# A decoder trunk step: the delta stage's projections, filler and head chain in another rank order, and the output branch's first banks

## The chip, the cores and the metric

The kernel runs on one core of one Trainium2 chip. The time is the device time of one execution in microseconds; three executions of the kernel before give a median of 2136.81 us (2132.54 to 2142.25). The engines are named as the profile names them: PE is TensorE (PEld its weight loads), DVE is VectorE, ACT is ScalarE, POOL is GpSimd and SP is SyncE, which issues most of the transfers.

## What is computed

One layer of a hybrid trunk for 1024 prompt tokens and 8 single-token samples, model width 1024, all in float32. Cut to what matters here:

```
h   = rmsnorm(x) * (1 + scale1) + shift1
qkv, gdn_gate, beta, a, sq, sk, sv, ga, gb = split(h @ w_in)

# gated delta rule, 8 heads of 128, chunks of positions, one after the other
q, k, v = silu(conv4(qkv))
for each head:
    T    = inverse(I + strictly_lower(beta k k^T * decay))      # per chunk
    for each chunk:                                             # a chain: S goes from chunk to chunk
        v_new = T (...v...) - T (...k...) S
        o     = q S + (q k^T * decay) v_new
        S     = S * last_decay + k^T v_new
y_a = (rmsnorm(o) * silu(gdn_gate)) @ w_gdn_out

o_b = sliding_window_attention(sq, sk, sv);  y_b = o_b @ w_swa_out
x   = x + gate1 * ((sigmoid(ga) * y_a + sigmoid(gb) * y_b) @ w_o)

h2  = rmsnorm(x) * (1 + scale2) + shift2
x   = x + gate2 * ((silu(conv3(h2 @ w_gate)) * (h2 @ w_up)) @ w_down)
y   = rmsnorm(x)
```

The states of the samples and the last rows of the caches are outputs too.

## The kernel before

**Products.** Every large product is made of three matmuls in a reduced float32 form: each operand is split into a high and a low part (`split`, L125: a copy on ACT, a subtraction on DVE), and `mm3` (L176) multiplies high by high, high by low and low by high (L178 to L180). A projection tile has 128 output columns. Its weights are loaded by SP (`load_split`, L130), and it runs over the 1032 tokens in three parts of 384, 384 and 264 columns; a part is 8 `mm3`, 24 matmuls, into one PSUM bank, which is then read out. `next_mm` (L172) goes round the list `self.mm` of bank pools: `pmm` has two banks and `pmf` one.

**Order.** Instructions carry a rank, `tc.cur_priority`, which counts up by one with each instruction that is written down. A planner puts each engine's instructions in order before the run: of those whose inputs and buffers are there in its own picture of time, it takes the one with the lowest rank. On the chip each engine then follows that fixed order. Buffers of one name in one pool are reused in the order in which the program asks for them. `issue_after` ties instructions of an engine behind a given one.

`weave` (L1248) writes several streams down one after the other but gives them overlapping ranks: a stream has a start and a step, and begins at the base `p` plus start. After each `yield`, a stream of step 1 counts on from where its instructions brought it, and a stream of another step is set to start plus so many steps. At the end the base for what follows is the largest rank that a counted stream has reached; before, streams with a start under 10000 are counted.

**The delta stage** (`run`, L1964 to L1982). For each of 8 heads one `weave` holds:

- `unit_inverse` (start 0, step 1): the triangular inverse of the head's 8 blocks. Transfers to DRAM and back (L987, L992, L1015, L1018), a loop of 15 pairs of small DVE operations (L1009, L1010), then rounds of small matmuls (L1028 to L1064) that write the tile `W`, of which there is one.
- `delta_scan` (100, step 1): 8 chunks, each a chain of three matmuls with ACT and DVE operations between them (L937 to L953). In the middle and at the end the output is normalized, turned and multiplied with the gate tile `sg`, which has one buffer for heads 0 to 6.
- `delta_prepare` of the next head (250, step 1): transposes, norms and the products of keys with keys and queries (L856 to L914).
- `head_projections`: for heads 0 to 5 the gate tile of head h (`delta_gate`, L840) and the three convolved tiles K, Q, V of head h+2 (`delta_project`, L784; `conv_tile`, L762). It is written behind two pieces of filler, as one stream with start 500 and step 100. All of it uses the two `pmm` banks.
- filler, `pieces` (L805): one piece is 8 steps of `self.filler`, one part of a tile. The filler is the 16 tiles of the two branch gates (`gates`, L1271; read out by L1284) and then an early piece of the output branch, 8 parts of 264 columns (`early_out`, L1294). Three pieces a head have start 10000 and step 100. Up to head 5 they use the bank `pmf` and a weight buffer of their own, of one copy.

Head 6 has three pieces and the gate tiles of heads 6 and 7 at start 500 in steps of 1, and nine more pieces at start 600; head 7 has what is left of the filler at start 600. From head 6 on filler and gates share `[pmm, pmm, pmf]`, and what is written after `delta_scan` is tied behind its steps by `spaced` (L164), two `mm3` to a step.

**The output branch** (`branches`, L1318) follows. Its products go round five banks, `[pmm, pmm, pmf, more, more]`, of which `more` is a new pool, laid where the delta stage's own small banks were. `turn`, the place in that round, is left as the delta stage had it. The first two products, j = 0 and 1 over the first 384 tokens, use rows that were loaded early.

**The second half** also has a `weave` (L1894): the output passes at step 1, and the states, norms and operands of the next part at steps of 10 to 120 with starts up to 730.

Of the kernel before, what the change touches and what calls it, by code (L numbers as in the profile page):

```python
# [62 lines left out]
class Step:  # L63
# [1184 lines left out]
    def weave(self, *streams):  # L1248

        tc = self.tc  # L1250
        p = end = tc.cur_priority
        for gen, start, step in streams:
            at = tc.cur_priority = p + start
            for _ in gen:
                if start < 10000:
                    end = max(end, tc.cur_priority)
                at += step
                tc.cur_priority = max(at, tc.cur_priority) if step == 1 else at
            if start < 10000:
                end = max(end, tc.cur_priority)  # L1260
        tc.cur_priority = end

# [661 lines left out]
    def run(self):  # L1924
        S, nc = ExitStack, self.nc
        self.constants()
        with S() as ca:
            with S() as c:
                pool, psum = self.pool("p2", 1, ctx=c), self.pool("q2", 1, PSUM, ctx=c)
                for tag, bufs in dict(qst=8, raw=2, kh=2, kl=2, E=3, obt=2, pp=2, pc=2, o=2).items():  # L1930
                    self.bufs[id(pool), tag] = bufs
                self.conditioning(pool, psum)
                self.vectors(pool, psum)
                self.h = self.new_parts()
                for lo in (8, 12, 0, 4):
                    self.modulation(pool, psum, "sc", lo, (("qst", 8),), "mrows")
                    if lo == 8:
                        self.junk = self.t(pool, [P, NP], "vch", bufs=1)
                        xs = self.norm_part(pool, self.load_rows(pool, 0, ("raw", "raw", "V")))
                    if lo == 12:  # L1940
                        self.a1 = self.norm_scale("a1", 8, self.n1w)
                        self.early = [self.win(COL_SK)]
                    if lo == 0:
                        self.early.append(self.win(COL_SQ))
                with self.tc.issue_after(self.mod_load.ins):
                    self.xs = {1: self.load_rows(pool, 1, ["qst"] * 3)}
                    self.junk = self.t(pool, [P, NP], "qst", bufs=8)
                    self.early.append(self.win(COL_SV, tags=("wmh", "wml"), home=pool))
                    self.early.append(self.win(COL_SQ + P, tags=("obt", "obt"), home=pool))
                self.xs[2] = self.load_rows(pool, 2, ("raw", "raw", "V"))  # L1950
                self.modulate_part(pool, psum, 0, xs, self.a1, 0)
                self.attention(pool, psum)
            cg = S()
            pgt = self.pool("pgt", 1, ctx=cg)
            self.pz, self.zs = self.pool("pz", 1, ctx=cg), True
            pg = self.pool("pg", 1, ctx=ca)
            self.fill_side = pg, 1, 1
            self.fill_where, self.gt = [self.fill_side], (pgt, "gt")
            with S() as c:
                pa, pool, psum = self.pool("pa", 1, ctx=c), self.pool("p4", 1, ctx=c), self.pool("q4", 1, PSUM, ctx=c)  # L1960
                self.W = self.t(pool, [P, NCH, P], "W", bufs=1)
                nc.gpsimd.memset(self.W, 0.0)
                self.kqv, self.sg = {}, {}
                self.weave((self.delta_project(pa, pool, 0), 0, 1))  # L1964
                self.weave((self.delta_prepare(pool, psum, 0), 0, 1), (self.delta_project(pa, pool, 1), 100, 1))
                for h in range(H):
                    if h + 2 == H:
                        self.fill_where, self.fill_psum = [self.fill_side, self.where], None
                        self.mm = [self.pmm, self.pmm, self.pmf]
                    prep = self.prep  # L1970
                    streams = [(self.unit_inverse(pool, psum, h, prep[0]), 0, 1),
                               (self.delta_scan(pool, psum, h, prep), 100, 1)]
                    if h + 2 < H:
                        streams[1:1] = [(chain(self.pieces(2), self.head_projections(pa, pool, h)), 500, 100)]
                        streams.append((self.pieces(3), 10000, 100))
                    else:
                        if h + 2 == H:
                            streams[1:1] = [(chain(self.pieces(3), *(self.delta_gate(pa, pool, i) for i in (h, h + 1))), 500, 1)]
                        streams.append((self.head_projections(pa, pool, h), 600, 100))
                    if h + 1 < H:  # L1980
                        streams.append((self.delta_prepare(pool, psum, h + 1), 250, 1))
                    self.weave(*streams)  # L1982
                    self.steps = []
                for _ in self.filler:
                    pass
            self.a2 = self.norm_scale("a2", 32, self.n2w)
        with S() as c:
            pool2, pool = self.pool("p6b", 1, ctx=c), self.pool("p6", 1, ctx=c)

            self.psm, more = self.pool("qs", 2, PSUM, ctx=c), self.pool("qb", 2, PSUM, ctx=c)  # L1990
            mm, self.mm = self.mm, [self.pmm, self.pmm, self.pmf, more, more]
            self.branches(pool, pool2)
            self.mm = mm
        cg.close()
        self.wctx.close()
        self.second_half()
# [40 lines left out]
```

## Time and profile before

| | us |
|---|---|
| median of three executions | 2136.81 (2132.54 to 2142.25) |
| profiled execution, its time | 2136.28 |
| its span, first to last instruction | 2134.5 |
| PE busy in the span | 2046.5 |
| DVE, ACT, POOL busy | 1393.5, 854.7, 534.6 |
| delta stage, about | 430 to 1155 |

Busy times are those of instructions on the engine; matmuls overlap each other, so a row's duration is longer than the distance from one start to the next. In a row of the timeline the text in brackets is the idle time just before the instruction and what ended it. In a row of a line's instructions stand the count, the least, median and greatest duration in ns, the first and the last start in us, and the shapes. A stretch's row has, for each engine, busy time and number of instructions, and then TensorE's granted clock as a share of full speed, the mean busy share of the DMA engines and the GB/s that they moved.

### The profile page before, as it was taken

Reading aid. Unit: us, or ns where it says so; the run is one execution under the profiler, and the core shown is the slowest. Engines: PE = TensorE matmul, PEld = TensorE weight load, DVE = VectorE, ACT = ScalarE, POOL = GpSimd, SP = SyncE. Lnnn points to the kernel's source line nnn. Section 1 sums busy time; section 2 is a strip of 40 time slices with the busy share of each in tenths; the row PEclk is TensorE's granted clock in tenths of the full one; section 3 lists DMA queues with packets and bytes.
Section 4 is the critical chain, followed back from the end, with each engine's and each line's share of the span. In section 5 each row is a group of like instructions: output and inputs, shape, how many; then the busy total and the mean of one; then the engine's idle time right before and its main releaser. Section 6 shows DMA issues by size and latency. Waiting matters only on the chain. (4 is left out here: it accounts for less than half of the span.)

```text
span 2134.5 us, 41210 instructions
## 1 busy us (share of the span) xinstructions
PE 2046.5 (96%) x16245; PEld 1935.3 (91%) x16245; DVE 1393.5 (65%) x2781; ACT 854.7 (40%) x2125; POOL 534.6 (25%) x592
## 2 busy tenths in 40 slices
PE   7999999999899999999989989998999999999898
PEld 4985888899899999999879989898999999999898
DVE  4756667465655736557445575479888788678866
ACT  3655445434244233443343222344343343343443
POOL 1000000020221211212110220003546546545531
PEclk8999999999999999999989999999999999999999
DMA  7256442141332322313166663622333333388972
GB/s 272 86 133 204 141 161 90 49 135 48 76 85 58 83 58 54 89 52 76 48 183 211 213 224 100 182 61 71 109 95 95 110 95 95 120 285 276 317 228 85
DMA packets 301821, 274.95 MB, mean 129 GB/s; under 512 B 59666, under 2 KB 248303, under 8 KB 301612
## 3 DMA queue, kind: packets, MB, share of 16 engines
q1 hardware_dynamic: 296140, 252.49, 38.6%
q0 software_dynamic: 5200, 19.32, 2.6%
q8 instruction: 127, 2.08, 0.4%
q14 instruction: 66, 0.54, 0.1%
q10 hardware_dynamic: 288, 0.52, 0.1%
HBM read 212.54 MB, written 62.12 MB: 129 GB/s over the span
## 5 line engine op out<-in xcount | busy, mean ns | idle before, releaser
L178 PE MATMUL mm<-b1h,wh 128*128 128x384 f32 (+1 forms) x1520 | 499.0, 329 | 5.9 <-ACT gt L1284 4.1
L180 PE MATMUL mm<-b1h,wl 128*128 128x384 f32 (+1 forms) x1520 | 491.4, 325 | 2.1 <-DVE wl L128 2.1
L179 PE MATMUL mm<-b1l,wh 128*128 128x384 f32 (+1 forms) x1520 | 490.8, 323 | 0.0
L178 PEld LDWEIGHTS mm<-b1h,wh 128*128 128x128 f32 x1520 | 287.8, 190 | 15.7 <-ACT gt L1284 6.2
L180 PEld LDWEIGHTS mm<-b1h,wl 128*128 128x128 f32 x1520 | 287.3, 189 | 7.9 <-issue 4.3
L179 PEld LDWEIGHTS mm<-b1l,wh 128*128 128x128 f32 x1520 | 288.0, 189 | 3.8 <-issue 3.5
L127 ACT ACTIVATE wh<-raw 128x1024 fp32r<-128x1024 f32 x83 | 87.0, 1048 | 135.7 <-PE mm L179 75.9
L128 DVE TENSOR_TENSOR wl<-raw,wh 128x1024 fp32r<-128x1024 f32 x82 | 100.8, 1229 | 48.8 <-ACT wh L127 47.9
L179 PE MATMUL mm<-pk,w 128*128 128x260 f32 (+1 forms) x440 | 124.3, 283 | 1.1 <-DVE pk L128 1.1
L178 PE MATMUL mm<-pk,w 128*128 128x260 f32 (+1 forms) x440 | 124.3, 283 | 0.0
L180 PE MATMUL mm<-pk,w 128*128 128x260 f32 (+1 forms) x440 | 124.2, 282 | 0.0
L128 DVE TENSOR_TENSOR w<-ws,w 128x512 fp32r<-128x512 f32 x88 | 74.1, 843 | 37.4 <-ACT w L127 37.4
L1609 ACT COPY bml<-mm 128x256 f32<-128x256 f32 (+1 forms) x132 | 49.2, 374 | 108.5 <-PE mm L180 101.8
L178 PE MATMUL mm<-bmh,w 128*128 128x260 f32 (+1 forms) x320 | 90.4, 283 | 0.9 <-DVE fa L1686 0.9
L180 PE MATMUL mm<-bmh,w 128*128 128x260 f32 (+1 forms) x320 | 90.3, 282 | 0.0
L180 PE MATMUL mm<-b2h,wl 128*128 128x384 f32 (+1 forms) x256 | 83.4, 329 | 4.5 <-DVE wl L128 4.5
L178 PE MATMUL mm<-b2h,wh 128*128 128x384 f32 (+1 forms) x256 | 83.8, 329 | 2.4 <-DVE t L1327 2.4
L179 PE MATMUL mm<-b2l,wh 128*128 128x384 f32 (+1 forms) x256 | 83.9, 328 | 0.4 <-DVE b2l L128 0.4
L179 PEld LDWEIGHTS mm<-pk,w 128*128 128x128 f32 x440 | 82.8, 188 | 1.3 <-DVE pk L128 1.3
L178 PEld LDWEIGHTS mm<-pk,w 128*128 128x128 f32 x440 | 82.8, 188 | 0.3 <-ACT bml L1609 0.2
L180 PEld LDWEIGHTS mm<-pk,w 128*128 128x128 f32 x440 | 83.0, 189 | 0.0
L127 ACT ACTIVATE w<-ws 128x512 fp32r<-128x512 f32 x88 | 55.4, 632 | 49.9 <-PE wv L180 45.0
(648 smaller groups left out, 5984.1 us busy)
## 6 DMA issues: line engine op xcount, KB each, us to landing
raw<-in_w_in_dram SPq DMA_DIRECT2D x60, 512.0 KB
ws<-in_w_ffn_down_dram SPq DMA_DIRECT2D x55, 256.0 KB
raw<-xd SPq DMA_DIRECT2D x47, 258.0 KB
raw<-in_w_ffn_down_dram SPq DMA_DIRECT2D x47, 256.0 KB
raw<-in_w_ffn_gate_dram SPq DMA_DIRECT2D x22, 512.0 KB
raw<-in_w_ffn_up_dram SPq DMA_DIRECT2D x22, 512.0 KB
qst<-in_w_mod_dram SPq DMA_DIRECT2D x16, 512.0 KB
raw<-in_w_mod_dram SPq DMA_DIRECT2D x16, 512.0 KB
```

The source lines that it names most:

```text
L127: self.nc.scalar.activation(hi, x, AF.Copy)
L128: (eng or self.nc.vector).tensor_tensor(lo, x, hi.bitcast(F32), op=ALU.subtract)
L178: mm(ps, whi, xhi, start=first, stop=False, **kw)
L179: mm(ps, whi, xlo, start=False, stop=False, **kw)
L180: self.last_mm = mm(ps, wlo, xhi, start=False, stop=last, **kw).ins
L1609: self.last_copy = nc.scalar.copy(r[p, i], x[p])
```

## The change

`weave` counts streams by their step instead of their start. In the delta stage five starts go to 100000: the projections' stream of heads 0 to 5 (with the two pieces at its front), the stream of three pieces and two gates of head 6, and the pieces of heads 6 and 7. Three pieces a head stay at 10000. The starts of the inverse, the scan and the preparation stay. Before the output branch `turn` is set to -1, so that its first product goes to the first bank of the list.

```diff
@@ weave
         for gen, start, step in streams:
             at = tc.cur_priority = p + start
             for _ in gen:
-                if start < 10000:
+                if step == 1:
                     end = max(end, tc.cur_priority)
                 at += step
                 tc.cur_priority = max(at, tc.cur_priority) if step == 1 else at
-            if start < 10000:
+            if step == 1:
                 end = max(end, tc.cur_priority)
@@ run
                     if h + 2 < H:
-                        streams[1:1] = [(chain(self.pieces(2), self.head_projections(pa, pool, h)), 500, 100)]
+                        streams[1:1] = [(chain(self.pieces(2), self.head_projections(pa, pool, h)), 100000, 100)]
                         streams.append((self.pieces(3), 10000, 100))
                     else:
                         if h + 2 == H:
-                            streams[1:1] = [(chain(self.pieces(3), *(self.delta_gate(pa, pool, i) for i in (h, h + 1))), 500, 1)]
-                        streams.append((self.head_projections(pa, pool, h), 600, 100))
+                            streams[1:1] = [(chain(self.pieces(3), *(self.delta_gate(pa, pool, i) for i in (h, h + 1))), 100000, 1)]
+                        streams.append((self.head_projections(pa, pool, h), 100000, 100))
...
-            mm, self.mm = self.mm, [self.pmm, self.pmm, self.pmf, more, more]
+            mm, self.mm, self.turn = self.mm, [self.pmm, self.pmm, self.pmf, more, more], -1
```

More of the change, by code (lines that the diff above doesn't have):

```diff
@@ L1977, in run @@
                         if h + 2 == H:
-                            streams[1:1] = [(chain(self.pieces(3), *(self.delta_gate(pa, pool, i) for i in (h, h + 1))), 500, 1)]
-                        streams.append((self.head_projections(pa, pool, h), 600, 100))
+                            streams[1:1] = [(chain(self.pieces(3), *(self.delta_gate(pa, pool, i) for i in (h, h + 1))), 100000, 100)]
+                        streams.append((self.head_projections(pa, pool, h), 100000, 100))
                     if h + 1 < H:
```

## The prediction

> **What bounds the kernel now.** I read the page first (busy shares, the slices of TensorE's clock), then the stretches of the delta stage, then what TensorE waited for there, then single places in the order of time. The page says that TensorE is the engine that counts:
>
> ```profile
> span 2134.5 us, 41210 instructions
> PE 2046.5 (96%) x16245; PEld 1935.3 (91%) x16245; DVE 1393.5 (65%) x2781; ACT 854.7 (40%) x2125; POOL 534.6 (25%) x592
> PEclk8999999999999999999989999999999999999999
> ```
>
> The change keeps every matmul, so only time in which TensorE stands still, or runs at a lower granted clock, can move. The edited stage runs from about 430 to 1155 us. By stretches (us; busy and count of PE, PEld, DVE, ACT, POOL; then granted clock, DMA share, GB/s):
>
> ```profile
> 430.00:540.00 110.00, 108.51 (x908) 106.29 (x907) 67.67 (x124) 42.33 (x123) 20.94 (x31) 1.00 0.33 91
> 540.00:570.00 30.00, 24.70 (x150) 23.17 (x148) 24.51 (x56) 8.64 (x22) 12.41 (x14) 0.94 0.38 95
> 570.00:1030.00 460.00, 452.31 (x4146) 437.55 (x4146) 264.93 (x566) 170.29 (x499) 81.51 (x120) 1.00 0.26 68
> 1030.00:1040.00 10.00, 7.30 (x43) 6.20 (x44) 4.13 (x9) 8.68 (x38) 1.30 (x2) 0.66 0.26 71
> 1040.00:1100.00 60.00, 59.78 (x525) 58.05 (x524) 31.26 (x90) 18.62 (x58) 12.63 (x20) 1.00 0.28 76
> 1100.00:1110.00 10.00, 5.22 (x84) 4.45 (x82) 6.31 (x8) 6.02 (x10) 1.77 (x2) 0.84 1.07 352
> 1110.00:1120.00 10.00, 6.47 (x44) 6.12 (x45) 1.66 (x3) 3.10 (x7) 0.00 (x0) 0.50 0.97 267
> 1120.00:1155.00 35.00, 34.32 (x275) 33.62 (x275) 19.73 (x39) 12.27 (x30) 4.57 (x6) 0.99 0.57 161
> sum 725.00, PE 698.61 PEld 675.44 DVE 420.21 ACT 269.95 POOL 135.14; mean PE 87.33 PEld 84.43 DVE 52.53 ACT 33.74 POOL 16.89
> ```
>
> Idle is 725 - 698.6 = 26.4 us. Where the clock is below 1, busy time times (1 - clock) is lost too: 24.70 x 0.06 = 1.5, 7.30 x 0.34 = 2.5, 5.22 x 0.16 = 0.8, 6.47 x 0.50 = 3.2 and 0.3 in the last row, 8.3 in all. So about 35 us, 1.6% of the time, is all that a better order can win. It is concentrated: 5.3 + 1.5 = 6.8 us at 540-570, 2.7 + 2.5 = 5.2 at 1030-1040, (4.8 + 3.5) + (0.8 + 3.2) = 12.3 at 1100-1120; the long steady part has 7.7 us in 460.
>
> Why 540-570 is thin: the gate projection of head 1 (L848 reads its three parts), the next convolution input (L770) and the filler (L1284):
>
> ```profile
> L848 ACT ACTIVATE th<-mm x3: 373/491/493, 533.6 to 614.4; 128x384 f32<-128x384 f32 x2, 128x264 f32<-128x264 f32 x1
> L770 ACT COPY z<-mm x1: 481/481/481, 620.4 to 620.4; 128x384 f32<-128x384 f32 x1
> L1284 ACT ACTIVATE gt<-mm x11: 372/482/493, 543.7 to 607.8; 128x384 f32<-128x384 f32 x7, 128x264 f32<-128x264 f32 x4
> ```
>
> Two parts of gate 1 are multiplied early and then sit in both projection banks until scan 0 gives `sg` back, so the third follows at 614; no projection runs meanwhile, and only filler, through one bank, is left. The gap at 1100-1120 is the other end of it: head 7's inverse comes after the gate filler has run out.
>
> ```profile
> 1103.57 0.28 PE L180 MATMUL mm<-b1h,wl 128*128 128x264 f32 x1
> 1108.00 1.45 PE L1051 MATMUL tp<-T,tmp 32*32 32x32 f32 x32 [4.15 <-ACT tmp L1048]
> 1112.19 1.94 PE L1060 MATMUL tp<-MR,UZ 64*64 64x64 f32 x16 [2.75 <-DVE MR L1057]
> 1114.80 1.96 PE L1064 MATMUL tp<-W,UZ 64*64 64x64 f32 x16 [0.67 <-ACT UZ L1061]
> 1117.43 0.80 PE L940 MATMUL rc<-vn,W 128*128 128x128 f32 x2 [0.67 <-ACT W L1065]
> ```
>
> **The chain of heads.** Starts of the eight inverses (L995), then the eight chunks of scan 5 and of scan 7 (L942; first and last start):
>
> ```profile
> L995 POOL COPY T<-unit x8: 289/292/294, 432.4 to 1032.1; 128x128 f32<-128x128 f32 x8
> L942 ACT ACTIVATE s<-rc,c x8: 362/368/375, 952.4 to 1030.1; 128x128 f32<-128x128 f32 x8
> L942 ACT ACTIVATE s<-rc,c x8: 358/368/369, 1118.3 to 1144.8; 128x128 f32<-128x128 f32 x8
> ```
>
> A head's period is (1032.1 - 432.4) / 7 = 85.7 us. Scan 5 takes 77.7 us for what scan 7, with far less beside it on VectorE, does in 26.5. `W` has one copy, so inverse h+1 can't finish before scan h; 77.7 and some 8 us of inverse make the whole period. The chain of small operations and TensorE's own work are of nearly one length, and at 1100 it is the chain that is late.
>
> **The change, part by part.**
>
> *Projections from +500 to +100000, no longer counted in the next base.* A head's base then grows by some 350 ranks, not 1100 (instructions counted in the code), so the small operations of heads 0 to 6 all stand ahead of every projection. Four tiles per head move. Each brings a load on SP, a split on ScalarE and VectorE, 72 matmuls and three copies; the three convolved ones also two small GpSimd operations, two tanh and six VectorE operations, three of them like L776:
>
> ```profile
> raw<-in_w_in_dram SPq DMA_DIRECT2D x60, 512.0 KB
> L776 DVE SCALAR_TENSOR_TENSOR K<-z,cw,K x21: 1266/1275/1287, 439.5 to 987.5; 128x1024 f32<-128x1024 f32 x21
> 551.03 0.34 PE L178 MATMUL mm<-b1h,wh 128*128 128x384 f32 x1
> 551.21 0.34 PE L179 MATMUL mm<-b1l,wh 128*128 128x384 f32 x1
> ...
> 1152.41 0.28 PE L179 MATMUL mm<-b1l,wh 128*128 128x264 f32 x1
> 1152.52 0.28 PE L180 MATMUL mm<-b1h,wl 128*128 128x264 f32 x1
> 1153.00 0.42 PE L178 MATMUL mm<-b1h,wh 128*128 128x384 f32 x1
> ```
>
> From start to start a matmul takes 0.18 us at 384 columns and 0.11 to 0.12 at 264: 24 x (0.18 + 0.18 + 0.12) = 11.5 us a tile, 3.8 us a filler part. None of it is added or removed. What moves ahead of it is the chain: on VectorE, the 15 pairs of the inverse now stand ahead of nine 1.28 us convolution steps a head, 11.5 us. SP's queue is passed by the inverse's loads as well; at a DMA share of 0.26 to 0.28 in the steady part I cost that at nothing, because weights have a second buffer and one tile hides 11.5 us of load. If that cover fails, the wait is again TensorE's.
>
> *Filler ahead of projections.* Three of five parts a head stand at +10000. The other two keep the front of the projections' chain, and filler shares one weight buffer and one bank, so parts run in program order: five parts of head h come before gate h and the tiles of h+2, then those of h+1. The price is order alone. For 540-570 it means that gate 1 comes behind up to 8 more filler parts, 8 x 3.8 = 30 us of the 80.8 between its first part and its third. I take half of 6.8: 3.5 us gained (bounds 0 and 6.8).
>
> *Steady part, 570-1030.* 7.7 us idle. With chunks no longer queued behind convolutions the chain runs ahead of TensorE, and projections stay in hand as cover; I take 2 us (bounds: a gain of 7.7, and the loss of the third case below).
>
> *Head 6 and 7.* Gates 6 and 7 with three parts go to +100000 in single steps, so head 7's base lies behind them; nine parts of head 6 and the early output parts go from +600 to +100000. Parts of head 6 stay tied behind scan 6's steps, those of the early output behind scan 7's, as before. At 1030-1040 both banks again wait for `sg`; with the chain ahead there are gates and parts to run: 4 us of 5.2 (bounds 0 and 5.2). At 1100-1120 the inverse of head 7 should be nearer its cover: after the last tile, 3 + 6 + 9 parts x 3.8 = 68 us and early output 64 x 3 x 0.12 = 23 us remain, 91 us and the small operations. Against it stands the chain of head 7: from the start of its inverse, 1032.1, to its scan, 1117.4, it took 85 us with its preparation and a hole of 13.6 us in it, so some 72 without the hole, and 26.5 of scan, 98 in all. That fits barely, so I take 8 of 12.3 (bounds 0 and 12.3).
>
> *The output branch's banks.* `turn = -1` puts its first two products into the two projection banks. In the rows above the first 384-column matmul follows the early output's last one after four transposes and no idle time; there is nothing to win in this order. A bank that comes free late would cost one part, 24 x 0.18 = 4 us, and cover of two parts may save 8: I take 0.
>
> *The other weave.* `end` now counts only streams of step 1, and the second half weaves too, with steps of 10 to 120: the first gate weights of the FFN and the last norm move up by some 450 ranks, ahead of the third norm's tail. There:
>
> ```profile
> 1450.00:1500.00 50.00, 43.86 (x352) 42.36 (x352) 47.57 (x67) 22.62 (x44) 24.88 (x23) 1.00 0.25 78
> ```
>
> 6.1 us idle, with VectorE at 95%: the same VectorE work in another order. I take 0 (bounds 6 either way).
>
> Sum: 3.5 + 2 + 4 + 8 = 17.5 us. The profiled execution took 2136.28 us (span 2134.5), 0.5 below the median: 2136.28 - 17.5 = 2118.8, against the median 2119.
>
> On the clock: the Trainium skill ("TensorE: Matmul & The Clock Gate", Part 1) says that TensorE falls to half rate after a window of about 3.4 us without work, and knows no value between. The 0.50 behind the 4.15 us gap agrees; the 0.66 at 1030-1040, where busy time is 7.3 of 10, would need such a gap and shows a thin stretch. By the rule alone the third term could be no more than its 2.7 us of idle time, and the sum would be 16.2.
>
> **The rivals.** What TensorE waited for between 430 and 1200 (total, times, longest):
>
> ```profile
> PE mm L178 <- ACT gt L1284: 4.1, 7, 1.3
> PE rc L940 <- DVE y L938: 1.8, 2, 1.1
> PE rc L944 <- ACT s L942: 1.6, 4, 0.6
> ```
>
> *The order hardly moves.* Projections wait for buffers that scans give back, filler for its one bank; program order within each buffer may leave the queue nearly as it is. For it: 452.31 busy of 460 in the steady part; against it: the banks held for 80 us. Then only about half of the first and third terms come, 2136 - 3 = 2133.
>
> *Small operations hold the queue.* TensorE takes its matmuls in order. A scan has 8 + 8 + 7 = 23 matmul steps that wait for ScalarE or VectorE, 184 in eight heads. Ranked above all else, each is put in as soon as the planner thinks its input is there; where the chip is later, everything behind waits. Now 6 of them wait, 3.4 us, 0.57 each. If a third (61) did, it would be 61 x 0.57 = 35 us, 2119 + 35 = 2154. It decides from 17.5 / 0.57 = 31 steps on. Against it: scans already ranked above their own head's projections, and waited 6 times. The Trainium skill ("PSUM — Partial Sum Buffer", Engine vs sequencer instructions) has the same rule, that matmuls start and finish in program order while weight loads may run ahead; the four gaps of the rows at 1108 to 1117 agree.
>
> *Head 7 comes later.* Filler that goes early can't cover late: if tile V of head 7 slips by the nine parts of head 6 (34 us) and the chain isn't ahead, the hole of 1117.4 - 1103.9 = 13.6 us grows to about twice itself: 2136 + 14 = 2150. For it: filler is now preferred to head 7's projections; against it: parts run in program order, so the same ones lie behind that tile.
>
> **How the numbers follow.** Forecast 0.46, own range 2104 (all of 6.8 + 7.7 + 5.2 + 12.3 = 32 us) to 2126 (10 us); order hardly moves 0.28; small operations hold the queue 0.16; head 7 later 0.10. A measurement of this kernel tells about 0.5%, 10.7 us, from no change. Faster by more is the forecast, 0.46; within it the second case, 0.28; slower the last two, 0.26. The range that should hold it 8 times in 10 is 2104 to 2150: it leaves out the upper part of the third case and little else.
>
> **What would show it.** Right: gate 1's three parts closer than 80.8 us; idle at 540-570 under 3 us; scans of the middle heads shorter than 77.7; no gap over 2 us between the last gate filler and the early output; 0.9 or more of clock in every stretch; the stage ends near 1137, and all after it is as long as before. Wrong: waits of L940 and L944 above 15 us together, or scan 7 beginning after 1117 with nothing beside it; or the second half, whose matmuls are the same, changing by more than 6 us.

## The result, and the profile after

The changed kernel takes 2124.68 us (median of six runs, 2121.29 to 2125.88), the kernel before 2134.27 beside it (2132.54 to 2142.25): a ratio of 0.9948, 95% interval 0.9931 to 0.9964. It is some 11 us faster (7.7 to 14.7). The prediction of 2119 had the direction and overstated the size.

One thing above is wrong. The diff in the section on the change, and the prediction's paragraph on heads 6 and 7, give head 6's stream of three pieces and two gates a step of 1. The change has step 100:

```diff
-                            streams[1:1] = [(chain(self.pieces(3), *(self.delta_gate(pa, pool, i) for i in (h, h + 1))), 500, 1)]
+                            streams[1:1] = [(chain(self.pieces(3), *(self.delta_gate(pa, pool, i) for i in (h, h + 1))), 100000, 100)]
```

So that stream isn't counted either, and head 7's base lies only some 350 ranks behind head 6's. The kernel as it was written there was run too, as e8.

The stretches of the changed kernel, with the same columns as the prediction's (engines' busy time and count, then granted clock, DMA share, GB/s); the 460 us from 570 also in four parts:

```profile
430.00:540.00 110.00, 108.33 (x912) 105.97 (x911) 60.91 (x116) 42.17 (x122) 22.10 (x33) 1.00 0.35 97
540.00:570.00 30.00, 30.00 (x203) 29.96 (x202) 22.38 (x57) 8.79 (x21) 11.54 (x14) 1.00 0.39 97
570.00:1030.00 460.00, 450.67 (x4122) 433.78 (x4120) 273.51 (x576) 174.40 (x507) 78.22 (x119) 0.99 0.25 66
570.00:930.00 360.00, 356.92 (x3318) 344.58 (x3316) 213.61 (x454) 135.37 (x397) 63.66 (x96) 1.00 0.26 69
930.00:950.00 20.00, 17.78 (x123) 16.03 (x116) 10.62 (x16) 11.55 (x39) 2.39 (x4) 0.84 0.11 31
...
1000.00:1030.00 30.00, 26.29 (x354) 24.33 (x352) 13.54 (x21) 10.12 (x22) 3.28 (x4) 1.00 0.20 57
1030.00:1040.00 10.00, 8.24 (x53) 7.51 (x54) 4.09 (x10) 8.46 (x43) 1.15 (x2) 0.66 0.34 111
1040.00:1100.00 60.00, 59.01 (x581) 56.46 (x580) 29.68 (x86) 17.01 (x50) 12.80 (x19) 1.00 0.25 64
1100.00:1110.00 10.00, 10.00 (x74) 9.55 (x72) 6.70 (x10) 6.70 (x11) 1.63 (x2) 1.00 0.94 305
1110.00:1120.00 10.00, 7.63 (x58) 6.82 (x56) 4.57 (x8) 3.26 (x5) 0.32 (x1) 1.00 1.19 307
1120.00:1155.00 35.00, 31.64 (x232) 30.39 (x233) 19.66 (x39) 12.63 (x30) 4.57 (x6) 1.00 0.75 224
```

540 to 570 is full, 1100 to 1110 is full; 1030 to 1040 is about as thin as it was; and there is a hole at 930 to 950 that the kernel before did not have there.

Rows of single lines in the changed kernel: the readouts of gate 1 (L848), the starts of the eight inverses (L995), and the chunks of scan 5 and of scan 7 (L942):

```profile
L848 ACT ACTIVATE th<-mm x3: 375/490/490, 571.1 to 620.6; 128x384 f32<-128x384 f32 x2, 128x264 f32<-128x264 f32 x1
...
L995 POOL COPY T<-unit x8: 289/289/291, 436.0 to 1029.8; 128x128 f32<-128x128 f32 x8
...
L942 ACT ACTIVATE s<-rc,c x8: 349/367/370, 950.2 to 1027.8; 128x128 f32<-128x128 f32 x8
...
L942 ACT ACTIVATE s<-rc,c x8: 349/367/369, 1107.2 to 1137.2; 128x128 f32<-128x128 f32 x8
```

Gate 1's parts lie 49.5 us apart instead of 80.8. From the first inverse to the last takes 593.8 us instead of 599.7, from there to the start of scan 7's last chunk 107.4 instead of 112.7. Scan 5 is as long as before. Scan 2 is not; its chunks in the kernel before and in the changed one:

```profile
L942 ACT ACTIVATE s<-rc,c x8: 348/368/371, 688.6 to 769.0; 128x128 f32<-128x128 f32 x8
...
L942 ACT ACTIVATE s<-rc,c x8: 349/367/367, 695.3 to 769.3; 128x128 f32<-128x128 f32 x8
```

Scan 2 takes 74.0 us instead of 80.4. From the start of head 3's inverse to that of the next it takes 84.2 us instead of 90.9; no other head became shorter by more than 2.5 us.

The rounds of head 7's inverse in the changed kernel (TensorE, in the order of time):

```profile
1084.62 0.54 PE L1034 MATMUL tp<-T,tmp 32*32 32x32 f32 x38
...
1087.35 0.69 PE L1046 MATMUL tp<-MR,U 32*32 32x32 f32 x32
...
1089.13 0.69 PE L1051 MATMUL tp<-T,tmp 32*32 32x32 f32 x30
...
1094.28 1.14 PE L1060 MATMUL tp<-MR,UZ 64*64 64x64 f32 x16
...
1100.80 0.56 PE L1064 MATMUL tp<-W,UZ 64*64 64x64 f32 x6
...
1105.43 0.38 PE L940 MATMUL rc<-vn,W 128*128 128x128 f32 x2
```

And in the kernel before, the two rounds whose distance matters:

```profile
1088.84 0.32 PE L1034 MATMUL tp<-T,tmp 32*32 32x32 f32 x14
...
1102.60 0.69 PE L1046 MATMUL tp<-MR,U 32*32 32x32 f32 x32
```

From L1034's last matmul to L1046 took 13.8 us before, with nothing idle: TensorE was multiplying filler that stood ahead in its order. It now takes 2.7 us, and filler is left to lie beside the later rounds. With it the idle 4.15 and 2.75 us of 1108 and 1112 are gone.

### The profile page after: what moved, and what is told of

It is laid out like the page before. It is cut to its first block, busy times and chain, and to the rows that moved or that the text cites. A ratio compares the mean times of both kernels' runs of the same rounds, so it can differ in the third digit from the quotient of the medians.

```text
span 2124.2 us, 41233 instructions
## 1 busy us (share of the span) xinstructions
PE 2046.7 (96%) x16245; PEld 1931.8 (91%) x16245; DVE 1396.3 (66%) x2781; ACT 853.8 (40%) x2125; POOL 533.8 (25%) x592
```

## The experiments

All ratios are to the kernel before, run beside each kernel. The last four columns come from each kernel's one profile: first to last inverse (L995), from there to the last chunk of scan 7 (L942), from there to the last readout of y_a (L1331), and the rest of the span.

| kernel | median us | ratio, 95% interval | heads 0-6 | tail | branches | rest |
|---|---|---|---|---|---|---|
| before | 2134.27 | | 599.7 | 112.7 | 183.3 | 806.4 |
| changed | 2124.68 | 0.9948 (0.9931 to 0.9964) | 593.8 | 107.4 | 181.9 | 805.1 |
| e12, changed again | 2123.97 | 0.9935 (0.9913 to 0.9958) | 595.5 | 108.9 | 182.9 | 802.9 |
| e1, banks alone | 2128.18 | 0.9973 (0.9959 to 0.9986) | 601.5 | 113.4 | 180.0 | 799.1 |
| e2, without banks | 2123.17 | 0.9947 (0.9929 to 0.9964) | 594.9 | 107.3 | 185.4 | 803.5 |
| e3, last heads as before | 2127.07 | 0.9960 (0.9947 to 0.9974) | 596.0 | 106.9 | 186.5 | 805.2 |
| e4, filler behind | 2135.57 | 1.0006 (0.9995 to 1.0017) | 609.2 | 109.7 | 181.6 | 800.2 |
| e5, filler ahead alone | 2136.06 | 1.0001 (0.9991 to 1.0011) | 604.5 | 113.7 | 183.9 | 801.5 |
| e8, head 6 in steps of 1 | 2117.46 | 0.9918 (0.9904 to 0.9933) | 595.4 | 108.7 | 181.3 | 799.6 |
| e9, count alone | 2126.90 | 0.9947 (0.9928 to 0.9967) | 602.7 | 108.0 | 184.8 | 801.5 |
| e10, gate 1 late | 2136.50 | 0.9988 (0.9976 to 1.0000) | 604.0 | 113.4 | 184.1 | 802.6 |
| e11, filler shifted | 2125.14 | 0.9938 (0.9917 to 0.9960) | 596.7 | 108.6 | 180.6 | 801.0 |

How far a column can be trusted: up to head 7's inverse e1 and e9 have the order of the kernel before, and heads 0 to 6 took 599.7, 601.5 and 602.7. The changed kernel's order gave 593.8, 595.5, 594.9 (e2) and 595.4 (e8). So one profile says a stretch to some 3 us.

**e1, the banks alone.**

```diff
 # kernel before
-            mm, self.mm = self.mm, [self.pmm, self.pmm, self.pmf, more, more]
+            mm, self.mm, self.turn = self.mm, [self.pmm, self.pmm, self.pmf, more, more], -1
```

> The kernel before with `turn = -1` alone. What the two traces show so far: from the first inverse to the end the changed kernel is 13.9 us shorter, 11.2 of it in the delta stage and the rest in the branch products behind it, where y_a's products lost 4.5 us and y_b's gained 3.1. Theory: the gain comes from the ranks in the delta stage, and the round of banks is worth nothing by itself: this kernel stands within 2 us of the one before. Rival: the waits at the head of y_a's products (2.4 us for a VectorE tile, 1.7 us for a weight load, clock 0.83) come from banks that are still busy, and the new round removes them: 4 to 5 us faster.

Faster by 3.0 to 8.7 us: more than the theory allows, and the rival's 4 to 5 us lie inside. The waits that the rival names did change. Without the new round (kernel before), at the start of y_a:

```profile
1237.97 0.41 PE L178 MATMUL mm<-b2h,wh 128*128 128x384 f32 x1 [2.35 <-DVE t L1327]
1238.74 0.45 PE L179 MATMUL mm<-b2l,wh 128*128 128x384 f32 x1 [0.36 <-DVE b2l L128]
```

With it (e1):

```profile
1245.65 0.44 PE L178 MATMUL mm<-b2h,wh 128*128 128x384 f32 x1 [1.54 <-ACT wh L127]
```

The wait for the readout of a product (L1327), read as a wait for its bank, gives way to one for weights. The branches are 3.3 us shorter, so the rival's reason can be behind a part of the gain; but the heads, in unchanged order, are 1.8 us longer, and up to the last readout of y_a the column sums of e1 are only 0.8 us below the kernel before, within the spread. The larger part, 7.3 us, stands in the last column, behind the products whose banks were changed. That column is taken up below.

**e2, the change without the banks.**

```diff
 # changed kernel
-            mm, self.mm, self.turn = self.mm, [self.pmm, self.pmm, self.pmf, more, more], -1
+            mm, self.mm = self.mm, [self.pmm, self.pmm, self.pmf, more, more]
```

> The changed kernel without `turn = -1`. Theory (ranks alone make the gain): it stays 9 to 10 us faster than the kernel before, within 2 us of the changed kernel, with its delta stage as long as there. Rival (half the gain is the banks'): 4 to 6 us faster than before only. Third: without the new round the first y_b product waits for the early output's last bank, one part of some 4 us, as the prediction bounded it.

The theory holds: the same time as the changed kernel, the same heads and tail. The branches are 2.5 to 3.5 us longer than in the two runs of the changed kernel, so by one profile each the new round is worth about that there. In the changed kernel it then repairs what the other order of the delta stage seems to cost the branches (183.3 before, 185.4 here).

**e3, the last heads as before.**

```diff
 # changed kernel
-    ... streams[1:1] = [(chain(self.pieces(3), ...gates...), 100000, 100)]
-    streams.append((self.head_projections(pa, pool, h), 100000, 100))
+    ... streams[1:1] = [(chain(self.pieces(3), ...gates...), 500, 1)]
+    streams.append((self.head_projections(pa, pool, h), 600, 100))
```

> The changed kernel with the streams of heads 6 and 7 as before (three pieces and gates 6, 7 at start 500 in steps of 1, the pieces of both heads at 600). Theory: heads 0 to 5 and the tail are two separate gains: idle time at 540 to 570 stays away (worth 6.8 us), while from the start of head 7's inverse to the end of scan 7 it takes the 112 us of the kernel before again instead of 107: about 5 to 7 us slower than the changed kernel, 3 to 4 faster than before. Rival: the tail gains because heads 0 to 5 left more filler and an earlier chain; then it stays within 2 us of the changed kernel.

The tail does not go back to 112: it stays at 106.9. So the 100000 of heads 6 and 7 is not what shortens it. Its interval overlaps that of the changed kernel; what its profile is longer by stands in the branches (186.5). Two things could keep the tail short: the order of heads 0 to 5, or `weave`, which here still counts by the step. e9 tells these apart.

**e4, filler behind the projections.**

```diff
 # changed kernel
-                        streams.append((self.pieces(3), 10000, 100))
+                        streams.append((self.pieces(3), 200000, 100))
```

> The changed kernel with the three pieces of a head ranked behind the projections (200000 in place of 10000). Theory: what fills 540 to 570 is that five parts of filler now lie ahead of gate 1, so that its two first parts no longer sit in both banks until scan 0 ends; with the filler behind, gate 1's first parts come at 534 to 545 again, its third at 610 to 620, and the idle time of some 5 us at 540 to 570 is back: 4 to 7 us slower than the changed kernel. Rival: the small operations ahead of everything do it, whatever comes first of the rest: no more than 2 us apart.

The whole gain is gone, and more than expected. Gate 1 and the stretch at 540, in e4:

```profile
L848 ACT ACTIVATE th<-mm x3: 391/492/493, 533.6 to 616.1; 128x384 f32<-128x384 f32 x2, 128x264 f32<-128x264 f32 x1
...
540.00:570.00 30.00, 26.26 (x169) 25.01 (x169) 21.93 (x57) 7.39 (x19) 9.47 (x14) 1.00 0.40 106
```

Gate 1 lies as it did before, 82.5 us apart, and 3.7 us are idle, where 6.8 were lost in the kernel before. The greater part is lost elsewhere: heads 0 to 6 together take 609.2 us.

**e5, filler ahead alone.**

```diff
 # kernel before, in weave and run
-                if start < 10000:
+                if start < 10000 and step:
-                        streams.append((self.pieces(3), 10000, 100))
+                        streams.append((self.pieces(3), 450, 0))
```

> The kernel before in which only the three pieces of a head are ranked ahead of the projections (start 450 with no step, not counted in the next base); the projections keep start 500, heads 6 and 7 and the banks are as before. With the filler behind, the changed ranks of the projections brought nothing (1.0006). Theory: filler ahead is the whole of what heads 0 to 5 gain: no idle time at 540 to 570, head 3 some 84 us long in place of 91, and 4 to 7 us faster than before. Rival: the filler fills only because the projections are far behind the small operations; with them at 500 it pushes its own head's tiles back and the chain with them: within 2 us of before or slower.

The stretch at 540 fills by 5.0 us, as the theory said:

```profile
540.00:570.00 30.00, 28.18 (x189) 27.48 (x187) 23.88 (x55) 10.40 (x24) 12.47 (x15) 1.00 0.41 99
```

and the time does not move, as the rival said: the sum of heads, tail and branches is 902.1 against 895.7 in the kernel before. Projections behind without filler ahead (e4) and filler ahead with the projections where they were (e5) each gain nothing; only together do heads 0 to 6 get shorter.

**e6 and e7, two buffers for `sg`,** in the kernel before and in the changed one.

```diff
-        sg = self.t(pool, [P, NT], "sg", bufs=1) if h + 1 < H else ...
+        sg = self.t(pool, [P, NT], "sg", bufs=2) if h + 1 < H else ...
-            e = self.t(pool, [P, 4, P], "ed", bufs=1)
+            e = self.t(pool, [P, 4, P], "UZ", bufs=1)
-                junk = self.t(pool, [P, P], "osq2", bufs=1)
+                junk = self.t(pool, [P, P], "osq", bufs=1)
-        w01 = self.t(pool, [32, NCH, 32], "w01", bufs=1)
+        w01 = self.t(pool, [32, NCH, 32], "U16", bufs=1)
```

> The kernel before with two buffers for the gate tile `sg` (room for it is made by letting three small tiles share the buffers of others). It tests the reading of 540 to 570: two parts of gate 1 are multiplied and then hold both projection banks until scan 0 gives `sg` back. Theory: with a second `sg` gate 1's three parts are read out within some 20 us of one another, projections run on, and the idle time at 540 to 570 and the clock lost there, 6.8 us, are gone: 4 to 7 us faster than before. Rival: the stretch lacks work whose inputs are there, whatever the banks hold: within 2 us of before, the idle time moved to another place of the same head.

> The changed kernel with two buffers for `sg`, made as in the run beside it. Idle and clock lost at 930 to 950 (5.4 us) and at 1030 to 1050 (5.2 us) are what is left there in the changed kernel. Theory: both are gates that hold the banks until a scan ends; with a second `sg` they go, 5 to 9 us faster than the changed kernel, 0.990 to 0.992 of the kernel before. Rival: at these two places the scan of the last heads is itself late and the banks don't matter: within 2 us of the changed kernel.

Ratios of 1.1056 (1.1036 to 1.1076) and 1.1074 (1.1050 to 1.1098): these two say nothing on `sg`. The starts of the inverses in e6:

```profile
L995 POOL COPY T<-unit x8: 289/290/292, 430.1 to 1239.6; 128x128 f32<-128x128 f32 x8
```

809.5 us for heads 0 to 6. The room for the second `sg` was taken from tiles of the preparation, the scan and the inverse, which now share buffers across heads. That a head which could begin inside the one before now has to wait for it is the likely reason, and wasn't shown. A second `sg` without that wasn't tried.

**e8, head 6's stream in steps of 1.**

```diff
 # changed kernel
-                            streams[1:1] = [(chain(self.pieces(3), ...gates...), 100000, 100)]
+                            streams[1:1] = [(chain(self.pieces(3), ...gates...), 100000, 1)]
```

> The changed kernel with the stream of three pieces and gates 6 and 7 at 100000 in single steps, so that it counts and the base of head 7 lies behind it, which is how the diff of the document had it by mistake (the change has step 100). Theory of the prediction's third rival: head 7's small operations then come behind gates 6 and 7 and the nine pieces of head 6, and the stretch from head 7's inverse to the end of scan 7 grows from 107 us by up to 13. Rival: the buffers and the ties behind scan 6 set the order there anyway: within 2 us of the changed kernel.

The tail does not grow, so the third rival is refuted for this form too. This is the fastest kernel of the study, 0.9918; its interval meets that of the changed kernel only at 0.9931 to 0.9933, and overlaps that of e12. TensorE's order is that of the changed kernel up to about the start of scan 7, and up to the last readout of y_a the columns sum to 885.4 us, between 883.1 and 887.3 of the two runs of the changed kernel. By the columns the difference is in the rest: 799.6 against 805.1 and 802.9.

**e9, the count alone.**

```diff
 # kernel before, in weave
-                if start < 10000:
+                if start < 10000 and start != 600:
```

> The kernel before in which only the count is changed, and only for the pieces of heads 6 and 7 (start 600): they no longer move the base of head 7, which in the kernel before lay behind nine pieces of head 6. In the kernel before, the last rounds of head 7's inverse take from 56.8 to 84.7 us after its first copy, with filler matmuls between them, in the changed kernel from 55.1 to 73.8. Theory: this one count is the whole gain of the tail; scan 7 begins some 77 us after head 7's first copy in place of 86, the tail from that copy to scan 7's end takes 107 us in place of 113, and the kernel is 4 to 7 us faster than before. Rival: the tail is shorter because the filler was used in another order in heads 0 to 5; then the tail stays at 112 us or more and the time within 2 us of before.

The theory holds for the tail: 108.0 us, scan 7 begins 75.2 us after head 7's first copy instead of 86.2:

```profile
L995 POOL COPY T<-unit x8: 289/291/293, 431.7 to 1034.4; 128x128 f32<-128x128 f32 x8
...
L942 ACT ACTIVATE s<-rc,c x8: 367/368/368, 1109.6 to 1142.4; 128x128 f32<-128x128 f32 x8
```

540 to 570 is as thin as before, 24.89 of 30 at a clock of 0.89. The time, 7.1 to 15.4 us faster, is more than the 4.7 of the tail. The profile has 4.9 more in the rest and gives 3.0 back in the heads and 1.5 in the branches. The execution that was profiled took 2130.48 us, 3.6 above the median of e9, so some of the gain in time isn't in this profile and isn't located.

**e10, gate 1 late.**

```diff
 # kernel before, head_projections
-            yield from self.delta_gate(pa, pool, h)
+            if h != 1:
+                yield from self.delta_gate(pa, pool, h)
             yield from self.delta_project(pa, pool, h + 2)
+            if h == 1:
+                yield from self.delta_gate(pa, pool, h)
```

> The kernel before in which head 1 alone writes its gate tile behind the three convolved tiles of head 3 in place of ahead of them. It tests, without other buffers, whether 540 to 570 is thin because two parts of gate 1 hold both projection banks until scan 0 ends at some 600. Theory: the gate's first parts come 30 us later, the convolved tiles run in between, and the 6.8 us lost at 540 to 570 are gone: 4 to 7 us faster than before, unless scan 1 then waits for its gate. Rival: no work is to be had there whatever the banks hold: idle time of 4 us or more at 540 to 570, within 2 us of before.

Three stretches of e10:

```profile
540.00:555.00 15.00, 15.00 (x106) 15.00 (x105) 10.27 (x20) 2.91 (x6) 6.83 (x8) 1.00 0.47 104
555.00:565.00 10.00, 6.66 (x31) 6.14 (x30) 7.53 (x21) 3.70 (x7) 1.57 (x3) 0.83 0.25 69
565.00:595.00 30.00, 30.00 (x379) 28.50 (x378) 11.10 (x28) 8.06 (x22) 4.04 (x5) 1.00 0.16 39
```

With the gate out of the way TensorE is full to 555, so the held banks were what thinned that part. A hole of 3.3 us then opens at 555 to 565, the longest wait in it 2.3 us for the low half of a weight tile. The time is 0 to 5 us below the kernel before. The hold is real, and removing it alone moves the hole.

**e11, filler shifted to head 5,** on top of e8.

```diff
-                        streams.append((self.pieces(3), 10000, 100))
+                        streams.append((self.pieces((3, 3, 2, 2, 2, 6)[h]), 10000, 100))
```

> The fastest kernel so far (the changed one with head 6's stream in single steps, 0.992 of before) with three pieces moved from heads 2, 3 and 4 (two in place of three each) to head 5 (six in place of three). With filler ahead the pieces of a head are used early: 7, 7, 5, 5, 5 parts are read out in the stretches of heads 0 to 4 and 2 in that of head 5, and 3 to 5 us are lost at 930 to 950 and again at 1000 to 1030. Theory: the holes of heads 5 and 6 are lack of filler; with three pieces more there they close, and heads 2 to 4 hide the smaller cover: 3 to 8 us faster than that kernel. Rival: heads 2 to 4 are bound by their chain of small operations without those pieces, and open as much as is closed: within 2 us, or slower.

No gain on e8, and 930 to 950 is as thin as there. It doesn't refute lack of filler, though: ranked ahead, the added pieces were used up before 870 us, and the readouts of L1284 in the stretch from there to 950 went from 1 in e8 to none. The pieces would have had to be held back, which wasn't tried.

**e12, the changed kernel again.**

> The changed kernel once more, to see how far its time and its stretches repeat. Up to the first inverse all kernels of this study have the same order of instructions, and took 430.1 to 436.0 us there, the changed kernel the most. Theory: that is the clock of one execution and not of the kernel; the stretch comes at 430 to 434 us this time, the median within 3 us of 2124.7, and single steps in the code of head 6 (2117.5 in the other run) are worth 3 to 5 us in the norm stage behind the branch products only. Rival: the long first stretch repeats, and belongs to the kernel.

The first stretch took 431.6 us instead of 436.0 in the same kernel: that was the execution. The ratios of the two runs agree.

**The rest of the span.** Behind the products nothing was edited, and yet the last column runs from 799.1 to 806.4. In the kernel before, the changed one and e3 (806.4, 805.1 and 802.9, 805.2) TensorE's order behind y_a's products is nearly one and the same; in all others the planner put it in another order there, after an edit some hundred us earlier or more. One wait follows the order: TensorE waits for the diagonal of the norm (L1488). In the kernel before and in the changed one:

```profile
PE nr L1489 <- DVE dg L1488: 2.8, 1, 2.8
```

```profile
PE nr L1489 <- DVE dg L1488: 3.1, 1, 3.1
```

It is 1.9 us in e12, 2.1 in e3, 0.7 to 1.4 in e2, e8, e9 and e10, and gone in e1, e4, e5 and e11. In those others the last column is 799.1 to 803.5, with the old order 802.9 to 806.4. The two ranges meet, in e2 and e12, so for a single kernel one profile does not tell them apart; taken together, an edit upstream seems to win some us here by a new order, and the change as it stands kept the old one. That the wait is the whole of this difference wasn't shown.

## Why the prediction was right, and where not

**540 to 570: predicted 3.5 of 6.8, got all of it.** The two parts of the working were right (filler ahead of gate 1; the three parts closer). That the row was priced at half was caution. Filler ahead alone brings 5.0 of it (e5), the projections behind alone 3.1 (e4). This is time of TensorE; the chain of heads is no sooner for it: from the first inverse to the third it is 163.2 us, 160.6 before.

**Steady part: predicted 2 us gained, measured 4.4 lost.** This is the step that failed. Idle time from 570 to 1030 is 460 - 450.67 = 9.3 us against 7.7, and the clock at 930 to 950 costs 17.78 x 0.16 = 2.8 more. It did not fail all along the row. Three parts of it in the kernel before:

```profile
570.00:930.00 360.00, 354.74 (x3183) 344.28 (x3184) 207.77 (x445) 133.14 (x393) 64.59 (x97) 1.00 0.26 69
930.00:950.00 20.00, 19.89 (x254) 18.36 (x253) 6.22 (x14) 8.84 (x26) 2.34 (x5) 1.00 0.17 48
...
1000.00:1030.00 30.00, 28.86 (x373) 27.27 (x371) 14.09 (x23) 10.42 (x21) 5.08 (x4) 1.00 0.23 61
```

From 570 to 930 idle time fell from 5.3 to 3.1 us, 2.2 us gained, as much as was forecast for the whole row. The loss is behind 930: 2.1 us of idle time and 2.8 of clock at 930 to 950, and 2.6 us of idle time at 1000 to 1030. "The chain runs ahead of TensorE" was one reason given for the gain, and it shows in scan 2 above all; scan 5 took 77.6 us against 77.7. "Projections stay in hand as cover" was the other, and this is what failed. The three parts of gate 5 in the changed kernel, their readout (L848) and their multiplication into `sg` (L849):

```profile
L848 ACT ACTIVATE th<-mm x3: 369/490/491, 928.0 to 959.3; 128x384 f32<-128x384 f32 x2, 128x264 f32<-128x264 f32 x1
L849 DVE SCALAR_TENSOR_TENSOR sg<-th,mm x3: 422/545/546, 954.3 to 960.5; 128x384 f32<-128x384 f32 x2, 128x264 f32<-128x264 f32 x1
```

The first two lie in both projection banks until 954, as those of gate 1 did at 540 to 570 in the kernel before, and TensorE starts no matmul of a projection or of filler from 940.5 to 955.2. The kernel before holds the banks there too (926 to 956), but reads out two filler parts meanwhile, at 937 and 944; in the changed kernel there is none between 877 and 1003. That is the reason of the prediction's third rival, filler that goes early can't cover late, two heads before the place that it named.

The wait itself is not new. The longest one at 930 to 950 stands at 771 in the kernel before (first row), and in the changed kernel at 944 (second) and no longer at 771:

```profile
771.78 1.56 PE L1064 MATMUL tp<-W,UZ 64*64 64x64 f32 x16 [1.61 <-ACT W L1055]
```

```profile
944.09 1.97 PE L1064 MATMUL tp<-W,UZ 64*64 64x64 f32 x16 [1.61 <-ACT W L1055]
```

At 771 filler parts were read out on both sides of it, at 766 and 773, so lack of filler is not shown to be the whole cause.

**1030 to 1040: predicted 4 of 5.2, measured 0.6.** 1.8 us idle and 8.24 x 0.34 = 2.8 of clock are still lost. Even the 0.6 is the edge of the row: the same steps come 2.3 us earlier now, and from 1020 to 1050 idle time and clock lose 6.8 us against 6.0. The reading that both banks wait for `sg` is borne out: gate 6's first two parts are read out at 1016 and 1022 in the changed kernel (1018 and 1024 before) and multiplied into `sg` at 1039 (1043 before). What failed is "there are gates and parts to run". In both kernels TensorE's longest wait there is for the inverse, with nothing else in its order meanwhile; first the kernel before, then the changed one:

```profile
1030.57 0.49 PE L944 MATMUL rc<-s,kd 128*128 128x128 f32 x2 [0.65 <-ACT s L942]
1032.89 1.97 PE L1064 MATMUL tp<-W,UZ 64*64 64x64 f32 x16 [1.61 <-ACT W L1055]
```

```profile
1028.27 0.49 PE L944 MATMUL rc<-s,kd 128*128 128x128 f32 x2 [1.20 <-ACT s L942]
1030.59 1.14 PE L1064 MATMUL tp<-W,UZ 64*64 64x64 f32 x16 [1.61 <-ACT W L1055]
```

The last round of the inverse stands in TensorE's order before its copies of `W` are there. At 949 in the kernel before the same step came without a wait, with other matmuls ahead of it. Ranks that put small operations first put nothing there.

**1100 to 1120: predicted 8 of 12.3, measured 7.5** (2.4 us left there, and 3.4 instead of 1.0 lost at 1120 to 1155). The size was nearly right and the reason incomplete. The prediction asked whether filler would reach as far as a chain of 98 us; the chain itself was long because head 7's rank base counted the nine pieces of head 6, so its rounds were queued behind them. e9 shows that this count alone makes the tail short, and e3 that the new starts of heads 6 and 7 aren't needed for it.

**Banks and the other weave: both predicted 0.** The banks are worth some 3 us in the branches (e1, e2), within the bounds given; the time of the changed kernel is the same without them. Built with the second half's base counted in the old way, the program is the same, instruction for instruction on every engine, so that part of the change does nothing. The rest of the span changed by 1.3 us, and 3.5 in e12, inside the 6 that were allowed.

The terms sum to 6.8 - 4.4 + 0.6 + 7.5 = 10.5 us in place of 17.5, against 7.7 to 14.7 measured. The time lies inside the forecast's 2104 to 2126, 1.3 us from its end, and that is in part luck: the surplus at 540 to 570 stands against two terms that did not come. Of the rivals, small operations that hold the queue left a trace and no more:

```profile
PE rc L944 <- ACT s L942: 4.2, 6, 1.2
PE rc L940 <- DVE y L938: 3.4, 5, 1.1
```

7.6 us in 11 waits against 3.4 in 6; it would have decided from 31 steps on. Head 7 came earlier and not later, so the third rival failed where it was put.

For e8, the kernel that the prediction's text described, 2119 was nearer (2117.46), but not for the prediction's reason: by the columns, what it has over the changed kernel is the new order behind the products.

**Left open:** why e9's time is better than its stretches (its tail and its rest account for 9.6 us, its heads and branches give 4.5 back, with heads of an unchanged order); whether filler held back, or a second `sg` that costs nothing else, would close the holes at 930 to 950 and 1030 to 1040; why scan 2 and head 3 in particular became shorter.

## What to carry to other kernels

Where ranks set the order, look at what moves the base of the next stage: a filler stream that is counted pushes the next critical chain behind itself, and one condition in the count was worth nearly the whole gain of the tail (4.7 of 5.3 us). Filler ranked early fills the first hole and is spent earlier, so look where it runs out before giving it a place. And when a planner makes the order, an edit can change stages far from it: compare stretch by stretch, and run the same kernel twice, before a few us are given to the edit.

## What the runs showed of the hardware

The granted clock falls to half behind a thin stretch and not only behind a long gap. The hole of the changed kernel at 940, in stretches of 2 us:

```profile
940.00:942.00 2.00, 1.53 (x11) 1.01 (x10) 1.37 (x3) 1.44 (x4) 0.10 (x1) 1.00 0.00 0
942.00:944.00 2.00, 0.48 (x4) 0.29 (x3) 0.35 (x1) 1.89 (x6) 0.29 (x1) 0.88 0.11 33
944.00:946.00 2.00, 1.91 (x17) 1.79 (x17) 0.18 (x2) 1.62 (x9) 0.00 (x0) 0.50 0.00 0
...
948.00:950.00 2.00, 1.91 (x9) 1.76 (x10) 1.29 (x3) 1.84 (x11) 0.00 (x0) 0.50 0.00 0
950.00:952.00 2.00, 1.92 (x15) 1.58 (x13) 1.07 (x3) 1.83 (x10) 0.00 (x0) 0.91 0.53 217
```

The longest single wait there is 1.61 us, and TensorE was busy for 2.01 of the 4 us from 940; still some 7 us at 0.50 follow, which cost some 3 us, more than the 2 us of idle time. The prediction took 0.66 at 1030 to 1040 for a value between; in stretches of 2 us it is 0.50 from 1032 to 1038 in the kernel before, and between 0.50 and 1.00 only in the two where it changes (0.93 and 0.86). The Trainium skill ("TensorE: Matmul & The Clock Gate", Part 1) gives the clock gate these two values and none between (the 13/16 that it names beside them is a limit for three or more busy cores of a die, and this kernel runs on one), and the trace agrees; its idle window of about 3.4 us would have to be met by a stretch that is half busy.
